# Expert loop of a product-key layer in a new order: the gathered rows are weighted and summed by one VectorE operation, input blocks are multiplied two blocks ahead

## Chip, cores and metric

One NeuronCore of a Trainium2 chip runs the whole program. The metric is the device time of one execution in microseconds (us), as the median over several runs. A span below is the time from the first to the last instruction of one profiled execution.

## What is computed

The reference is one layer of a mixing network over 512 tokens of width 1024 (with 256 context tokens ahead of it), followed by an expert layer and a final RMSNorm. The change touches the expert layer and nothing before it. Cut to that layer:

```python
def peer_ffn(u, w_q, sub_keys, u_tab, v_tab):      # 512 tokens, 16384 experts
    ...                                            # 128 experts idx and weights g for each token
    act = gelu(einsum('tkd,td->tk', u_tab[idx], t))
    return einsum('tk,tkd->td', g * act, v_tab[idx])
...
h = h + g2 * peer_ffn(u, ...)
return rmsnorm(h, final_g)
```

All arithmetic is float32. Each expert has one row of 1024 numbers in `u_tab` (dotted with the token) and one in `v_tab` (added to the token's result with its weight).

## The kernel before

**Two ways through the experts.** Three of the four groups of 128 tokens (TD = 384 tokens) take the dense way: all 16384 experts are multiplied, in 128 blocks `a` of 128 experts. For a block, TensorE computes `pu`, the product of the block's u rows with the 384 tokens; ScalarE applies gelu, giving `act`; VectorE multiplies by `gd`, the sparse matrix of routing weights; the product `ww` is then the stationary operand with which the block's v rows are added to six accumulators `pv` in PSUM (3 token groups by 2 halves). The fourth group of 128 tokens takes the sparse way: for each of its 128 slots `k`, a gather brings one row of u and v (2 x 1024 numbers) for each of the 128 tokens, VectorE dots the u half (`g_dot`), ScalarE applies gelu (`g_act`), VectorE multiplies by the routing weight (`g_weight`, a 128x1 operation), ScalarE scales the v half and GpSimd adds it to `accG` (`g_acc`). Then the next gather is issued on GpSimd's queue (`g_load`, 4 row buffers).

**Float32 by three products.** TensorE multiplies each float32 operand as a high part and a low part: `split` (lines 175 to 184) lets ScalarE write the high part (line 177) and VectorE subtract it from the full value (line 180, the low part). `mm3` issues three matmuls: high by high, low by high, high by low (lines 187 to 189). So a block costs 3 x 8 = 24 matmuls of 384 columns for `pu` and 3 x 6 = 18 of 512 columns for `pv`.

**Blocks done ahead.** The list `AHEAD` holds 70 of the 128 blocks, spread evenly. Their `act` was computed in earlier stages while TensorE had room and lies in DRAM (`act_d`); in the loop it is loaded as `acl`. The other 58 blocks compute `pu` in the loop. Two blocks outside `AHEAD` never follow each other; at eleven places two blocks of `AHEAD` do.

**Stage `weights_T`, about 955 to 1164 us.** It builds the routing matrix in 12 quarters of four steps each; a step makes one-hot operands on VectorE (`oi`, line 1557, and `ow`, line 1561), 16 small matmuls (`gdps`), and copies on ScalarE. Three steps of each quarter also run one u block ahead. The sparse way handles one slot per quarter here (slots 0 to 11).

**The expert loop, about 1169 to 2016 us.** It runs over the blocks `i` with the order on every engine fixed by the order of the calls (`manual_schedule`). In iteration `i` the kernel before calls: `e_load(i+4)` and `e_weights(i+2)` (loads on SP's queue; `gd` for four blocks at a time); for about one slot `k` in each iteration `g_dot`, `g_act`, `g_weight`; the splits of u block `i+2` and v block `i+1`; `e_u(i+1)` (the u product and its gelu); `e_w(i+1)` (times `gd`, and split); `g_acc(k)` and `g_load(k+4)`; and last `e_v(i)`. So the v product of block `i` in an iteration needs the `ww` made one iteration earlier, and that `ww` needs a `pu` computed in that same earlier iteration. The raw loads use a ring of 10 buffers, the split blocks a ring of 6, `acl` has 3 tiles, and `gd` alternates between two.

Of the kernel before, what the change touches and what calls it, by code (L numbers as in the profile page):

```python
# [7 lines left out]
F32 = mybir.dt.float32  # L8
# [4 lines left out]
AF = mybir.ActivationFunctionType  # L13
ALU = mybir.AluOpType
# [3 lines left out]
P = 128  # L18
# [132 lines left out]
def build(tc, A, out, dbg=None):  # L151
# [23 lines left out]
    def split(hi, lo, full, eng=None, lows=None):  # L175

        S.activation(hi, full, AF.Copy)  # L177

        def low():
            (eng or V).tensor_tensor(lo, full, hi.bitcast(F32), ALU.subtract)  # L180
        if lows is None:
            low()
        else:
            lows.append(low)
# [1021 lines left out]
        for t in range(NX):  # L1206
            out_mm(accs[t], w, kk, t, i == 0, False)
    ld, sp = {}, {}
    FIRST = [(0, 1), (1, 0), (1, 1), (2, 0)]

    def e_fetch(a, i):
        ld[a, i] = wload(A["peer_ut"][a] if i == 0 else A["peer_uv"][a * P:(a + 1) * P, D:2 * D])

    def e_split(a, i, eng=None, lows=None):
        sp[a, i] = wspl(ld[a, i], (KB, 2)[i], eng, lows)
# [301 lines left out]

    def g_act(k):
        S.activation(actG[:, k:k + 1], actG[:, k:k + 1], AF.Gelu)  # L1519

    def g_weight(k):
        V.tensor_tensor(wG[:, k:k + 1], actG[:, k:k + 1], gG[:, k:k + 1], ALU.mult)  # L1522

    def g_acc(k):
        row = rows.pop(k)
        S.activation(row[:, D:2 * D], row[:, D:2 * D], AF.Copy, scale=wG[:, k:k + 1])  # L1526
        if k:
            G.tensor_tensor(accG, accG, row[:, D:2 * D], ALU.add)  # L1528
        else:
            G.tensor_copy(accG, row[:, D:2 * D])  # L1530


    def slots_T(t):
# [15 lines left out]
    def weights_T(t):  # L1549
        for q8 in range(16):  # L1550
            if q8 % 4 == 0:
                stg = sg.tile([P, P, TQ], F32, name="stg")

            def tb(ap):
                return ap[:, t * 16 + q8].rearrange("p w (g c) -> p (w g) c", c=2).unsqueeze(2).broadcast_to([P, 8, P, 2])
            oi = gs2.tile([P, 2, 4, P, 2], F16, name="oi", bufs=3)
            V.tensor_tensor(oi.rearrange("p w g b c -> p (w g) b c"), iotaA.unsqueeze(1).broadcast_to([P, 8, P, 2]), tb(ixT), ALU.is_equal)  # L1557
            ob, oa = oi[:, 0], oi[:, 1]
            ow = gs2.tile([P, 2, 4, P, 2], F16, name="ow", bufs=3)
            for w in range(2):  # L1560
                V.tensor_tensor(ow[:, w], oa, tb(gwT)[:, w * 4:w * 4 + 4], ALU.mult)  # L1561
            oh, ol = ow[:, 0], ow[:, 1]
            for q4 in range(2):
                ps = psD.tile([P, 4, P], F32, name="gdps")
                for j in range(4):
                    tt = q4 * 4 + j
                    pr, c = tt // 2, tt % 2
                    PE.matmul(ps[:, j, :], ob[:, pr, :, c], oh[:, pr, :, c], start=True, stop=False)
                    PE.matmul(ps[:, j, :], ob[:, pr, :, c], ol[:, pr, :, c], start=False, stop=True)  # L1569
                t0 = q8 % 4 * 8 + q4 * 4  # L1570
                S.activation(stg[:, :, t0:t0 + 4].rearrange("p a t -> p t a"), ps, AF.Copy, scale=1.0 / GSCALE)  # L1571
            if q8 % 4 == 3:
                nc.scalar.dma_start(gd_d[t * 4 + q8 // 4], stg)
            if q8 in UQ:
                next(ahead, None)
            k = t * 4 + q8 // 4
            gq[0] = stg
            if q8 % 4 == 0:
                if k:
                    g_acc(k - 1)  # L1580
                    g_load(k + 3)
                g_dot(k)
            elif q8 % 4 == 1:
                g_act(k)
            elif q8 % 4 == 3:
                g_weight(k)

    UQ = (0, 1, 3, 4, 5, 7, 8, 9, 11, 12, 13, 15)

# [51 lines left out]
    gls = [gl]  # L1641
    psV = ep.ps("psV", bufs=1)
    accT = [[psV.tile([P, 512], F32, name=f"pv{t}{hf}") for hf in range(2)] for t in range(3)]
    ac, ww, gw, sqs, fss = {}, {}, {}, {}, {}

    def e_load(a):
        if a in AHEAD:
            ac[a] = gl.tile([P, TD], F32, name="acl")
            nc.sync.dma_start(ac[a], act_d[AHEAD.index(a)])
        elif (a, 0) not in ld:  # L1650
            e_fetch(a, 0)
        if (a, 1) not in ld:
            e_fetch(a, 1)

    def e_split_u(a):
        if (a, 0) not in sp:
            e_split(a, 0)

    def e_split_v(a):
        if (a, 1) not in sp:  # L1660
            e_split(a, 1)

    def e_weights(a):
        if a % 4 == 0:
            n = NQ if a else NQ - 1
            gd = gls[a // 4 % 2].tile([P, NQ, 4 * TQ], F32, name="gd", bufs=1)
            nc.sync.dma_start(gd[:, 0:n, :], gd_d[0:n, :, a:a + 4, :].rearrange("q b a t -> b q (a t)"))
            if n < NQ:
                G.tensor_copy(gd[:, n, :], gq[0][:, 0:4, :].rearrange("p a t -> p (a t)"))
            gq[0] = gd  # L1670
        gd = gq[0][:, :, a % 4 * TQ:(a % 4 + 1) * TQ]
        gw[a] = gd

    def e_u(a):
        if a in AHEAD:
# [3 lines left out]
        S.activation(ac[a], pu[:, :TD], AF.Gelu)  # L1679

    def e_w(a):
        x = ac.pop(a)
        xq = x.rearrange("p (q t) -> p q t", q=NQ)
        V.tensor_tensor(xq, xq, gw.pop(a), ALU.mult)  # L1684
        wh = ex.tile([P, TD], F32R, name="wwh", bufs=3)
        wl = ex.tile([P, TD], F32R, name="wwl", bufs=3)
        split(wh, wl, x)
        ww[a] = (wh, wl)

    def e_v(a, t, hfs=(0, 1)):  # L1690
# [52 lines left out]
    def within(f, i):  # L1743
        if 0 <= i < P:
            f(i)
    LAST = 3
    kG = [12 + min(P - 12, (i * (P - 12) + 121) // 122) for i in range(P + 1)]
    with tc.manual_schedule():
        e_weights(0)
        sgp.close()  # L1750
# [2 lines left out]
        g2r = e1.tile([P, D], F32, name="g2r")  # L1753
        fgr = e1.tile([P, D], F32, name="fgr")
        hx = e1.tile([P, NX, D], F32, name="hx")
        for i in range(-4, P + 1):
            within(e_load, i + 4)
            if i > -2:
                within(e_weights, i + 2)
            now = range(kG[i], kG[i + 1]) if 0 <= i < P else ()  # L1760
            for k in now:
                g_dot(k)
                g_act(k)
                g_weight(k)
            within(e_split_u, i + 2)
            within(e_split_v, i + 1)
            within(e_u, i + 1)
            within(e_w, i + 1)
            for k in now:
                g_acc(k)  # L1770
                g_load(k + 4)
            if 0 <= i < P - LAST:
                for t in range(3):
                    e_v(i, t)
                del ww[i]
            if i == 64:
                f_load()
            if i == P - 4:
                f_mul(3, 0)
                f_mul(3, 1)  # L1780
            if i == P - 3:
                f_sq(3, 0)
                f_sq(3, 1)
                f_gain(3, 0)
                f_gain(3, 1)
            if i == P - 1:
                S.activation(e1.tile([P, 1], F32, name="warm"), epsc, AF.Sqrt)
# [49 lines left out]
```

## Time and profile before

| what | value |
|---|---|
| time, median of 3 runs (lowest to highest) | 2030.38 us (2030.21 to 2032.35) |
| the profiled execution's own time | 2030.01 us |
| its span | 2028.2 us |
| TensorE matmul busy | 1887.1 us (93%) |
| VectorE busy | 1516.8 us (75%) |
| ScalarE busy | 932.7 us (46%) |
| GpSimd busy | 914.9 us (45%) |
| mean DMA rate over the span | 220 GB/s |

PE is TensorE's matmuls, PEld its weight loads (they overlap), DVE VectorE, ACT ScalarE, POOL GpSimd, SP the engine that issues most loads. Matmuls are pipelined and the profile models their ends, so the busy share of PE hides short waits: the start times in the timeline tell more than the share does. The mean of a whole run also mixes stages with different limits; the change acts from about 955 us on. The profiled execution's time is 1.8 us above its span, and 0.4 us below the median of the runs.

### The profile page before, as it was taken

The numbers are of one execution on the slowest core, as the hardware profiler recorded it, in microseconds if no ns is written. First come the engines' busy times: TensorE is split into PE (matmuls) and PEld (weight loads), VectorE is DVE, ScalarE is ACT, GpSimd is POOL, SyncE is SP. The second block draws the span as 40 slices with busy tenths as digits, with TensorE's granted clock in tenths as the row PEclk, the third lists the DMA queues.
The fourth block names the chain that finished last, engine by engine and source line by source line (L and its number), as shares of the span: only waits on it lengthen the run. The fifth ranks groups of instructions, "written<-read, shape, count | busy, mean of one in ns | idle before, by whom it ended". The sixth has DMA issues, their size and how long they took to land.

```text
span 2028.2 us, 26813 instructions
## 1 busy us (share of the span) xinstructions
PE 1887.1 (93%) x9703; PEld 1546.4 (76%) x9703; DVE 1516.8 (75%) x2604; ACT 932.7 (46%) x1491; POOL 914.9 (45%) x458
## 2 busy tenths in 40 slices
PE   7999998879998999888999799999999999999997
PEld 4777866556777889888999677777787878778775
DVE  5552179986535456998899878888888888888885
ACT  4332233426544333433777645455445445444444
POOL 1004046740013543564122256576666575675653
PEclk9999999989999999989999789999999999999999
DMA  9546232145313433464787698888888998888971
GB/s 339 166 135 206 63 114 63 42 153 185 96 65 107 147 113 107 132 229 136 246 291 281 230 381 308 313 311 315 304 318 316 354 330 303 317 318 294 323 268 59
DMA packets 209044, 445.20 MB, mean 220 GB/s; under 512 B 13296, under 2 KB 135920, under 8 KB 190960
## 3 DMA queue, kind: packets, MB, share of 16 engines
q1 hardware_dynamic: 171616, 258.47, 39.0%
q0 software_dynamic: 18432, 134.23, 17.4%
q10 hardware_dynamic: 18864, 50.80, 6.7%
q8 instruction: 76, 1.25, 0.2%
q14 instruction: 56, 0.46, 0.1%
HBM read 394.02 MB, written 51.51 MB: 220 GB/s over the span
## 4 chain that ended last, share of the span: by engine, by line
PE 36%; DVE 29%; issue 17%; ACT 8%; DMA 6%; POOL 3%; ACTq 0%; DVEq 0%; SPq 0%; POOLq 0%
DVE wl L180 10%; DVE row L1516 6%; PE acc L187 4%; PE acc L189 4%; PE acc L188 4%; PE pu L189 3%; PE pu L187 3%; PE pu L188 3%; POOL wl L180 3%; ACT wwh L177 3%; DMA wraw<-in_peer_ut 2%; DVE oi L1557 2%; ACT wh L177 2%; DVE ow L1561 1%; PE acc L419 1%
## 5 line engine op out<-in xcount | busy, mean ns | idle before, releaser
L1528 POOL TENSOR_TENSOR accG<-accG,row 128x1024 f32<-128x1024 f32 x127 | 358.7, 2825 | 383.8 <-ACT row L1526 379.3
L180 DVE TENSOR_TENSOR wl<-wraw,wh 128x1024 fp32r<-128x1024 f32 x268 | 339.5, 1283 | 149.0 <-ACT wh L177 140.4
L177 ACT ACTIVATE wh<-wraw 128x1024 fp32r<-128x1024 f32 x324 | 335.1, 1051 | 227.3 <-PE acc L188 80.0
L189 PE MATMUL pu<-u2h,wl 128*128 128x384 f32 (+2 forms) x1040 | 360.9, 347 | 15.1 <-DVE wl L180 12.7
L187 PE MATMUL pu<-u2h,wh 128*128 128x384 f32 (+2 forms) x1040 | 359.3, 346 | 16.0 <-ACT act L1303 14.6
L188 PE MATMUL pu<-u2l,wh 128*128 128x384 f32 (+2 forms) x1040 | 354.8, 341 | 0.0
L187 PE MATMUL pv<-wh,wwh 128*128 128x512 f32 x768 | 310.0, 404 | 25.1 <-ACT wwh L177 24.8
L189 PE MATMUL pv<-wh,wwl 128*128 128x512 f32 x768 | 309.7, 403 | 0.0
L188 PE MATMUL pv<-wl,wwh 128*128 128x512 f32 x768 | 303.7, 395 | 0.0
L1522 DVE TENSOR_TENSOR wG<-actG,gG 128x1 f32<-128x1 f32 x128 | 223.2, 1744 | 33.0 <-ACT actG L1519 33.0
L1511 POOL DMA_INDIRECT row<-in_peer_uv,idxG x128 | 210.9, 1648 | 36.2 <-POOL accG L1528 33.1
L189 PEld LDWEIGHTS pu<-u2h,wl 128*128 128x128 f32 x1040 | 199.8, 192 | 32.2 <-DVE wl L180 28.1
L180 POOL TENSOR_TENSOR wl<-wraw,wh 128x1024 fp32r<-128x1024 f32 x56 | 143.7, 2570 | 166.3 <-ACT wh L177 139.6
L187 PEld LDWEIGHTS pu<-u2h,wh 128*128 128x128 f32 x1040 | 200.3, 193 | 20.2 <-ACT act L1303 15.9
L187 PEld LDWEIGHTS pv<-wh,wwh 128*128 128x128 f32 x768 | 144.9, 189 | 76.6 <-ACT wwh L177 49.7
L188 PEld LDWEIGHTS pu<-u2l,wh 128*128 128x128 f32 x1040 | 200.2, 193 | 2.5
L189 PEld LDWEIGHTS pv<-wh,wwl 128*128 128x128 f32 x768 | 144.7, 188 | 48.5 <-DVE wwl L180 16.6
L188 PEld LDWEIGHTS pv<-wl,wwh 128*128 128x128 f32 x768 | 144.9, 189 | 29.6 <-issue 0.2
L1516 DVE CUSTOM_DVE_ANT_0 row<-row,u2G 128x1024 f32<-128x1024 f32 x128 | 156.1, 1219 | 0.0
L1526 ACT ACTIVATE row<-row,wG 128x1024 f32<-128x1024 f32 x128 | 145.7, 1138 | 4.7 <-ACT act L1303 3.8
L177 ACT ACTIVATE wwh<-acl 128x384 fp32r<-128x384 f32 x70 | 36.7, 525 | 197.0 <-DVE acl L1684 197.0
L1571 ACT ACTIVATE stg<-gdps 128x512 f32<-128x512 f32 x96 | 96.8, 1137 | 17.7 <-PE gdps L1569 17.3
(412 smaller groups left out, 3346.0 us busy)
## 6 DMA issues: line engine op xcount, KB each, us to landing
wraw<-in_peer_ut SPq DMA_DIRECT2D x128, 512.0 KB, 4.6
wraw<-in_peer_uv SPq DMA_DIRECT2D x128, 512.0 KB, 6.3
gd_d<-stg ACTq DMA_DIRECT2D x12, 2048.0 KB, 8.4
gd<-gd_d SPq DMA_DIRECT2D x31, 768.0 KB, 9.1
wraw<-in_w_in SPq DMA_DIRECT2D x36, 512.0 KB, 4.1
acl<-act_d SPq DMA_DIRECT2D x70, 192.0 KB, 5.6
act_d<-act ACTq DMA_DIRECT2D x68, 192.0 KB, 3.8
kT<-in_ada_w SPq DMA_DIRECT2D x18, 512.0 KB, 4.6
```

The source lines that it names most:

```text
L177: S.activation(hi, full, AF.Copy)
L180: (eng or V).tensor_tensor(lo, full, hi.bitcast(F32), ALU.subtract)
L187: PE.matmul(ps, ah, bh, start=start, stop=False)
L188: PE.matmul(ps, ah, bl, start=False, stop=False)
L189: PE.matmul(ps, al, bh, start=False, stop=stop)
L1511: G.indirect_dma_start(out=rows[k], out_offset=None, in_=A["peer_uv"], in_offset=bass.IndirectOffsetOnAxis(ap=idxG[:, k:k + 1], axis=0))
L1516: V.tensor_tensor_reduce(row[:, 0:D], row[:, 0:D], u2G, 1.0, 0.0, ALU.mult, ALU.add, actG[:, k:k + 1])
L1522: V.tensor_tensor(wG[:, k:k + 1], actG[:, k:k + 1], gG[:, k:k + 1], ALU.mult)
L1526: S.activation(row[:, D:2 * D], row[:, D:2 * D], AF.Copy, scale=wG[:, k:k + 1])
L1528: G.tensor_tensor(accG, accG, row[:, D:2 * D], ALU.add)
L1557: V.tensor_tensor(oi.rearrange("p w g b c -> p (w g) b c"), iotaA.unsqueeze(1).broadcast_to([P, 8, P, 2]), tb(ixT), ALU.is_equal)
L1571: S.activation(stg[:, :, t0:t0 + 4].rearrange("p a t -> p t a"), ps, AF.Copy, scale=1.0 / GSCALE)
```

## The change

The sparse way loses three operations and gets others. VectorE no longer multiplies the 128x1 weight; ScalarE does, as a copy with a per-partition scale, right behind its gelu. ScalarE no longer scales the 1024-wide v half and GpSimd no longer adds it: one VectorE `scalar_tensor_tensor` multiplies the v half by the weight and adds `accG`. GpSimd keeps only the gathers. The slots are spread over 121 iterations in place of 122.

The loop gets a new order. u blocks (or `acl`) are loaded 6 iterations ahead, v blocks still 4, `gd` 5 in place of 2. u blocks are split at `i+3` in place of `i+2`, and `e_u` multiplies block `i+2` in place of `i+1`. `e_w(i+1)` comes first in the iteration, ahead of the dot. All high parts of an iteration are called before its low parts, which VectorE now does in the order ww, u, v. The list `FIRST`, the pieces that are loaded and split before the loop, no longer holds u block 2 (which is in `AHEAD`, so it was never multiplied) but u block 3.

```diff
-    FIRST = [(0, 1), (1, 0), (1, 1), (2, 0)]
+    FIRST = [(1, 0), (0, 1), (3, 0), (1, 1)]
...
     def g_act(k):
         S.activation(actG[:, k:k + 1], actG[:, k:k + 1], AF.Gelu)
-
-    def g_weight(k):
-        V.tensor_tensor(wG[:, k:k + 1], actG[:, k:k + 1], gG[:, k:k + 1], ALU.mult)
+        S.activation(wG[:, k:k + 1], actG[:, k:k + 1], AF.Copy, scale=gG[:, k:k + 1])
 
     def g_acc(k):
         row = rows.pop(k)
-        S.activation(row[:, D:2 * D], row[:, D:2 * D], AF.Copy, scale=wG[:, k:k + 1])
         if k:
-            G.tensor_tensor(accG, accG, row[:, D:2 * D], ALU.add)
+            V.scalar_tensor_tensor(accG, row[:, D:2 * D], wG[:, k:k + 1], accG, ALU.mult, ALU.add)
         else:
-            G.tensor_copy(accG, row[:, D:2 * D])
+            V.tensor_scalar(accG, row[:, D:2 * D], wG[:, k:k + 1], None, ALU.mult)
...
                 g_dot(k)
             elif q8 % 4 == 1:
                 g_act(k)
-            elif q8 % 4 == 3:
-                g_weight(k)
...
-    def e_load(a):
-        if a in AHEAD:
+    def e_load(a, i):
+        if i == 0 and a in AHEAD:
             ac[a] = gl.tile([P, TD], F32, name="acl")
             nc.sync.dma_start(ac[a], act_d[AHEAD.index(a)])
-        elif (a, 0) not in ld:
-            e_fetch(a, 0)
-        if (a, 1) not in ld:
-            e_fetch(a, 1)
+        elif (a, i) not in ld:
+            e_fetch(a, i)
...
+    def e_high(a, i):
+        if (a, i) in ld and (a, i) not in sp:
+            lows[a, i] = []
+            e_split(a, i, None, lows[a, i])
+
+    def e_low(a, i):
+        for f in lows.pop((a, i), ()):
+            f()
...
     def e_w(a):
         x = ac.pop(a)
         ...
-        split(wh, wl, x)
+        lows[a, 2] = []
+        split(wh, wl, x, None, lows[a, 2])
...
-        for i in range(-4, P + 1):
-            within(e_load, i + 4)
-            if i > -2:
-                within(e_weights, i + 2)
+        for i in range(-6, P + 1):
+            within(lambda a: e_load(a, 0), i + 6)
+            within(lambda a: e_load(a, 1), i + 4)
+            if i > -5:
+                within(e_weights, i + 5)
             now = range(kG[i], kG[i + 1]) if 0 <= i < P else ()
+            within(e_w, i + 1)
             for k in now:
                 g_dot(k)
+            within(lambda a: e_high(a, 0), i + 3)
+            within(lambda a: e_high(a, 1), i + 1)
+            within(lambda a: e_low(a, 2), i + 1)
+            within(lambda a: e_low(a, 0), i + 3)
+            within(lambda a: e_low(a, 1), i + 1)
+            for k in now:
                 g_act(k)
-                g_weight(k)
-            within(e_split_u, i + 2)
-            within(e_split_v, i + 1)
-            within(e_u, i + 1)
-            within(e_w, i + 1)
+            within(e_u, i + 2)
             for k in now:
                 g_acc(k)
                 g_load(k + 4)
```

## Rows read from the trace of the kernel before

**Rows 1.** Busy by stretch, 1200 to 1950 us: pu's instructions, then pv's.

```profile
1200.00:1950.00 750.00, 237.83 (x1232) 215.11 (x1230) 25.76 (x54) 1.00 0.89 316
...
1200.00:1950.00 750.00, 506.15 (x2050) 376.80 (x2051) 0.00 (x0) 1.00 0.89 316
```

**Rows 2.** Timeline of PE (start us, us long): first, some middle and last rows.

```profile
1169.33 0.79 PE L187 MATMUL pv<-wh,wwh 128*128 128x512 f32 x1 [7.24 <-ACT wwh L177]
...
1187.79 0.40 PE L187 MATMUL pv<-wh,wwh 128*128 128x512 f32 x1
...
1196.19 0.34 PE L187 MATMUL pu<-u2h,wh 128*128 128x384 f32 x1
...
1200.41 0.40 PE L187 MATMUL pv<-wh,wwh 128*128 128x512 f32 x1
...
2015.33 0.40 PE L189 MATMUL pv<-wh,wwl 128*128 128x512 f32 x1
```

**Rows 3.** Waits of PEld, 1200 to 1950 us: total us, times, longest.

```profile
PEld pv L187 <- ACT wwh L177: 36.8, 52, 2.0
PEld pu L189 <- DVE wl L180: 23.4, 44, 0.6
PEld pv L189 <- DVE wwl L180: 15.4, 52, 0.3
```

**Rows 4.** Timeline of DVE, ACT and POOL around 1500 us.

```profile
1497.30 1.99 ACT L177 ACTIVATE wh<-wraw 128x1024 fp32r<-128x1024 f32 x2
...
1499.37 2.35 DVE L180 TENSOR_TENSOR wl<-wraw,wh 128x1024 fp32r<-128x1024 f32 x2
...
1503.25 1.22 DVE L1516 CUSTOM_DVE_ANT_0 row<-row,u2G 128x1024 f32<-128x1024 f32 x1
...
1503.87 2.86 POOL L1528 TENSOR_TENSOR accG<-accG,row 128x1024 f32<-128x1024 f32 x1 [2.46 <-ACT row L1526]
...
1504.75 2.00 DVE L1522 TENSOR_TENSOR wG<-actG,gG 128x1 f32<-128x1 f32 x1 [0.27 <-ACT actG L1519]
...
1506.68 1.21 DVE L180 TENSOR_TENSOR wl<-wraw,wh 128x1024 fp32r<-128x1024 f32 x1
...
1507.00 1.71 POOL L1511 DMA_INDIRECT row<-in_peer_uv,idxG  x1 [0.27 <-POOL accG L1528]
...
1507.81 0.55 DVE L1684 TENSOR_TENSOR act<-act,gd 128x384 f32<-128x384 f32 x1
...
1508.39 0.53 ACT L177 ACTIVATE wwh<-act 128x384 fp32r<-128x384 f32 x1 [2.34 <-DVE act L1684]
...
1508.95 0.56 DVE L180 TENSOR_TENSOR wwl<-act,wwh 128x384 fp32r<-128x384 f32 x1 [0.59 <-ACT wwh L177]
```

**Rows 5.** Lines 1522, 585 and 1519 by themselves: duration ns min/median/max, first and last start.

```profile
L1522 DVE TENSOR_TENSOR wG<-actG,gG x128: 151/2007/2025, 973.7 to 1967.8; 128x1 f32<-128x1 f32 x128
...
L585 DVE SCALAR_TENSOR_TENSOR c<-xp,colv,c x12: 1015/1022/1023, 66.0 to 171.1; 128x770 f32<-128x770 f32 x12
...
L1519 ACT ACTIVATE actG<-actG x128: 192/203/207, 973.5 to 1967.5; 128x1 f32<-128x1 f32 x128
```

**Rows 6.** Timeline of a quarter of weights_T.

```profile
1110.46 3.44 DVE L1557 TENSOR_TENSOR oi<-iotaA,ixT 128x2048 f16<-128x2048 f16 x1
...
1128.03 2.49 POOL L1528 TENSOR_TENSOR accG<-accG,row 128x1024 f32<-128x1024 f32 x1 [13.30 <-ACT row L1526]
...
1128.16 3.44 DVE L1557 TENSOR_TENSOR oi<-iotaA,ixT 128x2048 f16<-128x2048 f16 x1
...
1132.39 0.23 PE L1568 MATMUL gdps<-ow,oi 128*128 128x128 f16 x1 [0.47 <-DVE ow L1561]
1132.98 0.22 PE L1569 MATMUL gdps<-ow,oi 128*128 128x128 f16 x1 [0.36 <-DVE ow L1561]
```

**Rows 7.** DMA: a stretch with more traffic, and us to landing of v loads.

```profile
1600.00:1700.00 100.00, 97.27 (x441) 79.33 (x440) 86.56 (x97) 51.17 (x76) 68.13 (x31) 1.00 0.94 340
...
wraw<-in_peer_uv SPq DMA_DIRECT2D x106, 512.0 KB, 6.3
```

More of the change, by code (lines that the diff above doesn't have):

```diff
@@ L1643, in build @@
     accT = [[psV.tile([P, 512], F32, name=f"pv{t}{hf}") for hf in range(2)] for t in range(3)]
-    ac, ww, gw, sqs, fss = {}, {}, {}, {}, {}
-    def e_load(a):
-        if a in AHEAD:
+    ac, ww, sqs, fss = {}, {}, {}, {}
+    def e_load(a, i):
+        if i == 0 and a in AHEAD:
             ac[a] = gl.tile([P, TD], F32, name="acl")
             nc.sync.dma_start(ac[a], act_d[AHEAD.index(a)])
-        elif (a, 0) not in ld:
-            e_fetch(a, 0)
-        if (a, 1) not in ld:
-            e_fetch(a, 1)
[L1655 to L1661, printed above, removed]
+        elif (a, i) not in ld:
[7 more added lines that the diff above has]
+            f()
+    lows = {}
+    gds = {}
     def e_weights(a):
@@ L1665, in e_weights @@
             n = NQ if a else NQ - 1
-            gd = gls[a // 4 % 2].tile([P, NQ, 4 * TQ], F32, name="gd", bufs=1)
+            gd = gds[a // 4] = gls[a // 4 % 2].tile([P, NQ, 4 * TQ], F32, name="gd", bufs=1)
             nc.sync.dma_start(gd[:, 0:n, :], gd_d[0:n, :, a:a + 4, :].rearrange("q b a t -> b q (a t)"))
@@ L1669, in e_weights @@
                 G.tensor_copy(gd[:, n, :], gq[0][:, 0:4, :].rearrange("p a t -> p (a t)"))
-            gq[0] = gd
-        gd = gq[0][:, :, a % 4 * TQ:(a % 4 + 1) * TQ]
-        gw[a] = gd
     def e_u(a):
@@ L1683, in e_w @@
         xq = x.rearrange("p (q t) -> p q t", q=NQ)
-        V.tensor_tensor(xq, xq, gw.pop(a), ALU.mult)
+        V.tensor_tensor(xq, xq, gds[a // 4][:, :, a % 4 * TQ:(a % 4 + 1) * TQ], ALU.mult)
         wh = ex.tile([P, TD], F32R, name="wwh", bufs=3)
         wl = ex.tile([P, TD], F32R, name="wwl", bufs=3)
-        split(wh, wl, x)
+        lows[a, 2] = []
+        split(wh, wl, x, None, lows[a, 2])
         ww[a] = (wh, wl)
@@ L1746, in build @@
     LAST = 3
-    kG = [12 + min(P - 12, (i * (P - 12) + 121) // 122) for i in range(P + 1)]
+    kG = [12 + min(P - 12, (i * (P - 12) + 120) // 121) for i in range(P + 1)]
     with tc.manual_schedule():
```

## The prediction, made before the changed kernel was seen

> **What bounds the kernel now.** I read the page's share of each engine first, then the stretches, then PE's timeline and its waits, and last the other engines' timelines inside one pair of iterations. The page calls PE 93% busy, which suggests that nothing is left; the start times say otherwise. From 1187.79 to 1196.19 us PE starts 36 pv matmuls with no wait, 0.2333 us each; from 1196.19 to 1200.41 it starts 24 pu matmuls, 0.1758 us each [rows 2]. Between 1200 and 1950 us it issues 1232 pu and 2050 pv matmuls [rows 1]: 1232 x 0.1758 + 2050 x 0.2333 = 216.6 + 478.3 = 694.9 us of work in 750. So 55.1 us, 7.3%, is lost there, at a granted clock of 1.00, that is 2.4 GHz [rows 1]. The reader is to see that PE is the bound and yet is kept waiting in nearly every pair of iterations. The weight loads name three causes: the high part of ww (ScalarE), the low part of a u block, the low part of ww (both VectorE) [rows 3]. (Their waits add up to more than 55 us, since a weight load starts ahead of the matmul before it has ended.)
>
> Why they are late stands in the timeline [rows 4]. After the dot, VectorE issues the 128x1 weight, and it lasts 2.00 us, until GpSimd's 2.86 us addition ends at 1506.73; alone it takes 0.15 [rows 5]. Behind it in VectorE's queue stand the low parts, and behind these the multiplication of a fresh `act`: 1507.81 us, with ww's high part at 1508.39 and its low part at 1508.95, where PE already waits. It is a chain inside one iteration: pu, gelu, product, high, low, pv.
>
> **The change, part by part.**
>
> *VectorE, sparse way.* Each slot loses the 2.00 us weight and gains a 1024-wide `scalar_tensor_tensor`. The trace of before has none of that size. The nearest is 770 wide, 1.02 us [rows 5]; adding 254 elements at the 1.04 ns per element of that row's neighbours (a 1024-wide low part takes 1.21 us against 0.56 for 384, so 0.65 / 640 = 1.02 ns) gives 1.28 us. Lower bound 1.21 (the plain 1024-wide subtraction), upper bound 1.21 + 1.85 = 3.06, if it were blocked as the weight is. I take 1.29: the 770-wide row is the same instruction form, and GpSimd has no additions left that could block it. So VectorE gains about 0.7 us per slot.
>
> *ScalarE* loses a 1024-wide scaling, about the 1.0 us of a 1024-wide high part [rows 4], and gets a 128x1 copy near the 0.20 us of its gelu [rows 5]. ScalarE has room either way; this counts as nothing, hidden beside VectorE's 1.29 us.
>
> *GpSimd* keeps the 1.71 us gather issue [rows 4], now behind VectorE's sum. The row it fetches is dotted four slots later, over 20 us away.
>
> *One block more of distance.* In the new order PE in iteration i needs only what the others made in iteration i-1 from a pu of iteration i-2. I lay out a pair of iterations, the first with a u block: PE 4.22 + 18 x 0.2333 = 8.42, then 4.20, together 12.62 us. VectorE's next iteration starts with the product of that u block's `act`, so at 4.22 + 0.47 (a gelu as long as the 384-wide ScalarE row, 0.53 at most) + about 0.2 = 4.9 us. Its work per iteration by [rows 4]: product 0.55, dot 1.22, ww low 0.56, v low 1.21, sum 1.29 = 4.83, and 1.21 more for a u block: 10.87 us in a pair, 86% of 12.62. Meanwhile ScalarE makes ww high (0.53), u high and v high (1.0 each) while VectorE dots, so each low part finds its high part ready or 0.1 us short. The u low part is ready at 4.9 + 0.55 + 1.22 + 0.56 + 1.21 = 8.4 us; PE wants it at 12.62. The ww of that iteration is ready before 8, wanted at 16.8. VectorE ends its second iteration at 4.9 + 10.87 = 15.8 and is let go again at 17.5. So every wait of [rows 3] has at least 4 us of cover, and where two blocks of `AHEAD` follow each other VectorE has 15.7 us of work in PE's 16.8. If the sum costs over 1.29 + (12.62 - 10.87) / 2 = 2.16 us the cover is gone and VectorE sets the pace.
>
> *Loads on SP.* u loads and `acl` are issued 6 ahead, `gd` 5, v 4 as before. With 3 `acl` tiles, the load for block i+6 waits until VectorE has taken the tile of about three `AHEAD` blocks earlier, in iteration i-1 or i, and v and `gd` loads stand behind it. `gd` waits for its tile's last product, also in i-1. That leaves a v load about three iterations, 19 us, against a median of 6.3 to land [rows 7]: nothing, with 12 us of cover. The bytes stay; in a loop 7% shorter 316 GB/s [rows 1] becomes 340, which the stretch from 1600 us already carried at a DMA share of 0.94 with PE undisturbed [rows 7]. `FIRST` trades one useless u block for u block 3: one load and one split fewer in the loop, about 1 us of VectorE, hidden.
>
> *Sum for the loop.* 55.1 us in the window. The stage runs from 1169.33 to 2015.73 us [rows 2], 96 us of it outside the window; at the same 7.3% that is 7.0. Total 62, of which I leave 2 for the start: the first pv matmuls last 0.79 instead of 0.40 us [rows 2] at 1.2 GHz after an idle PE, since the first ww hangs on loads that the change does not touch. Saved: 60 us, 64 if the edges lose more than the middle, 30 if half of the waits come back elsewhere.
>
> *Stage weights_T.* GpSimd's addition blocks one `oi` in a quarter: 3.44 us, its end set by the addition's end at 1130.5 [rows 6]; about 1.22 is its own (other steps), so 2.2 are lost. PE then waits 0.47 + 0.36 = 0.83 us for `ow` [rows 6]. VectorE gets 1.29 instead, earlier in the quarter, where the row of `ow` has about 1 us to spare. So 0.83 comes back in some 8 quarters of 17.7 us, 6.6 us, and about 0.9 in one of the two last ones, where only VectorE sets the pace (2.2 - 1.29): 7.5. Bounds 0 (the wait moves to the step behind the sum) and 12 (0.9 or a little more in all twelve).
>
> *One rule against one row.* The weight's 2.00 us beside 0.15 alone, ending with GpSimd's addition, shows that VectorE can be held for a whole GpSimd instruction [rows 4, 5]. The low part that ran from 1506.68 beside the gather issue of 1507.00 took its usual 1.21 us [rows 4], so the issue holds nothing. The Trainium skill (SBUF — State Buffer, section "Who interferes with whom") says that a VectorE instruction with two SBUF inputs contends with a GpSimd instruction that reads SBUF, and that the later one blocks fully. For the weight the trace agrees. Taken strictly for the gather issue too, which reads its indices from SBUF, it would give the last rival below, 2041 us, in place of the 1963 that the low part's row gives.
>
> *Total.* 2028.2 - 60 - 7.5 = 1960.7 us of span; 1.8 around it gives 1962.5, and the median stood 0.4 above the profiled run: **1963 us**.
>
> **The rivals.**
>
> *Half the waits return* (12%). A queue is in order, so a late gelu on ScalarE holds the next high part, and a late dot holds both. Against it: 4 us of cover. If half of the 62 stays: 1963 + 30 = 1993 us.
>
> *Loads become the wait* (5%). For it: a DMA share of 0.89 already [rows 1], and SP held by three `acl` tiles. Against it: 340 GB/s at 0.94 [rows 7]. If 316 GB/s were the ceiling the loop could not shrink at all and only weights_T's 7.5 would show: 2030.4 - 7.5 = 2023 us.
>
> *Slower: VectorE held by the gather issue* (3%). Each issue follows the sum, just where VectorE starts the next product, which has two SBUF inputs. Were it held for the 1.71 us, a pair would be 10.87 + 3.42 = 14.3 us, less about 0.07 of overlap for each of eleven starts (two low parts in 2.35 where one takes 1.21 [rows 4]) = 13.5, against 846.4 / 64 = 13.2 now. The loop would take 64 x 13.5 = 864, 18 us more: 2030.4 + 18 - 7.5 = 2041 us. It turns slower than before from a hold of about 1.5 us. Against it: the undisturbed low part above.
>
> **How the numbers follow.** The forecast holds 80%: its own range is 1950 (edges and weights_T at their best: 2030.4 - 66 - 12, and 2 for the start) to 1977 (weights_T at 0, loop 53). Adding the first rival up to 1993 brings the range to 1950 to 1993, with some 1 in 10 left out above and little below. I call 0.2%, 4 us, about what a measurement of this kernel can tell from no change. Faster holds the forecast, the half and most of the loads' case (at 2023 us it is 0.36% faster): 80 + 12 + 3 = 95%. Same: the rest of the loads' case, 2%. Slower: 3%.
>
> **What would show it.** Right: PE starts from the loop's second block on at 0.233 and 0.176 us with no waits of weight loads on wwh, wl or wwl; VectorE about 85% busy with gaps in front of the product of a fresh `act`; its sum near 1.29 us; DMA near 340 GB/s; quarters of weights_T near 16.8 us; loop near 786 us. Wrong: the sum above 2.16 us, or lengthened beside a gather issue; PE waiting for DMA; PE's granted clock below 1.00 in the loop; quarters still at 17.7.

## The result, and the profile after

The changed kernel takes **1978.86 us** (median of 4 runs, 1975.43 to 1979.52) against 2030.78 us for the kernel before on the same chip: a ratio of 0.974, 95% interval 0.9723 to 0.9757. The prediction said 1963 us and 1950 to 1993. The saving is 51.9 us where 67 were expected, and the stages show that this is not one shortfall but several differences, one of them the other way (spans of the profiled executions, us):

| stage | before | after | change | predicted |
|---|---|---|---|---|
| to the first `oi` of weights_T | 957.9 | 961.1 | +3.1 | 0 |
| weights_T, first `oi` to last `gdps` | 203.8 | 206.5 | +2.7 | -7.5 |
| PE idle before the first pv | 7.55 | 16.67 | +9.1 | 0 |
| loop, first pv to the end of the last | 846.4 | 780.5 | -65.9 | -60 |
| end of the last pv to the end of the span | 12.5 | 12.0 | -0.5 | 0 |

The first row is not the change's: up to there all fourteen kernels of this case run the same instructions, and their profiled executions take 955.1 to 964.5 us for them (956.1 and 956.6 in two that have the new sparse way). In weights_T the five kernels with the old sparse way take 203.8 to 204.9 us, and the six with that of the kernel after 205.8 to 206.9.

First the loop. Busy time by stretch of the kernel after: pu's instructions (PE, PEld, ACT, then granted clock, DMA share, GB/s), then pv's; and below a stretch of all engines (PE, PEld, DVE, ACT, POOL):

```profile
1200.00:1900.00 700.00, 229.72 (x1252) 221.52 (x1252) 26.82 (x54) 1.00 0.93 343
...
1200.00:1900.00 700.00, 487.11 (x2058) 385.69 (x2057) 0.00 (x0) 1.00 0.93 343
```

```profile
1500.00:1600.00 100.00, 100.00 (x470) 85.79 (x469) 80.15 (x104) 41.42 (x81) 15.81 (x17) 1.00 0.98 367
```

Counted as in [rows 1]: 1252 x 0.1758 + 2058 x 0.2333 = 700.2 us of work in 700. Nothing is lost any more. The waits of PEld between 1200 and 1900 us, all of them, beside [rows 3]:

```profile
PEld pu L187 <- ACT g2r L1093: 0.7, 1, 0.7
PEld pu L1091 <- issue: 0.5, 2, 0.2
```

The three releasers of [rows 3] are gone. DMA carries 367 GB/s at a share of 0.98 with PE full, above the 340 of [rows 7].

A pair of iterations on VectorE and ScalarE in the kernel after (timeline), beside [rows 4]:

```profile
1505.88 0.55 DVE L1680 TENSOR_TENSOR acl<-acl,gd 128x384 f32<-128x384 f32 x1
1506.35 1.22 DVE L1516 CUSTOM_DVE_ANT_0 row<-row,u2G 128x1024 f32<-128x1024 f32 x1
...
1506.52 0.53 ACT L177 ACTIVATE wwh<-acl 128x384 fp32r<-128x384 f32 x1 [2.59 <-DVE acl L1680]
...
1507.49 0.55 DVE L180 TENSOR_TENSOR wwl<-acl,wwh 128x384 fp32r<-128x384 f32 x1
1508.03 2.36 DVE L180 TENSOR_TENSOR wl<-wraw,wh 128x1024 fp32r<-128x1024 f32 x2
1510.30 1.28 DVE L1525 SCALAR_TENSOR_TENSOR accG<-row,wG,accG 128x1024 f32<-128x1024 f32 x1
...
1513.64 1.23 DVE L180 TENSOR_TENSOR wl<-wraw,wh 128x1024 fp32r<-128x1024 f32 x1
1514.78 1.28 DVE L1525 SCALAR_TENSOR_TENSOR accG<-row,wG,accG 128x1024 f32<-128x1024 f32 x1
1518.27 0.56 DVE L1680 TENSOR_TENSOR act<-act,gd 128x384 f32<-128x384 f32 x1 [2.21 <-ACT act L1674]
```

ScalarE makes ww's high part while VectorE dots, so `wwl` starts with no wait; VectorE's only gap, 2.21 us here, is in front of a fresh `act`, where the prediction put it. The sum by itself (duration ns min/median/max), beside [rows 5]:

```profile
L1525 DVE SCALAR_TENSOR_TENSOR accG<-row,wG,accG x127: 1276/1279/1282, 1002.1 to 1915.1; 128x1024 f32<-128x1024 f32 x127
```

1.279 us against the 1.29 predicted, and 1.282 at most.

Now what went the other way. A quarter of weights_T in the kernel after (timeline), beside [rows 6]:

```profile
1104.80 3.96 ACT L1568 ACTIVATE stg<-gdps 128x512 f32<-128x512 f32 x4
...
1109.16 1.06 ACT L177 ACTIVATE wh<-wraw 128x1024 fp32r<-128x1024 f32 x1 [0.40 <-ACT stg L1568]
...
1110.26 1.23 DVE L180 TENSOR_TENSOR wl<-wraw,wh 128x1024 fp32r<-128x1024 f32 x1 [2.50 <-ACT wh L177]
1111.40 1.28 DVE L1525 SCALAR_TENSOR_TENSOR accG<-row,wG,accG 128x1024 f32<-128x1024 f32 x1
1112.60 1.22 DVE L1516 CUSTOM_DVE_ANT_0 row<-row,u2G 128x1024 f32<-128x1024 f32 x1
...
1113.74 1.22 DVE L1554 TENSOR_TENSOR oi<-iotaA,ixT 128x2048 f16<-128x2048 f16 x1
```

No `oi` is held any more, but the sum now stands right behind a low part that waits 2.50 us for ScalarE, and the dot, `oi` and `ow` follow it. The quarters in the middle last 18.2 us (dot to dot) instead of 17.7; the last two get shorter, 14.5 and 12.2 us against 15.6 and 13.1. And the start of the loop (timelines of POOL, SP, DVE and PE):

```profile
1167.56 0.94 POOL L1511 DMA_INDIRECT row<-in_peer_uv,idxG  x1 [8.06 <-DVE accG L1525]
...
1167.93 0.38 SPq L1665 DMA_DIRECT2D gd<-gd_d  x1
...
1183.10 0.56 DVE L1680 TENSOR_TENSOR acl<-acl,gd 128x384 f32<-128x384 f32 x1 [15.81 <-DMA acl<-act_d]
...
1184.27 0.80 PE L187 MATMUL pv<-wh,wwh 128*128 128x512 f32 x1 [16.36 <-ACT wwh L177]
```

The gather for slot 15 goes out 0.4 us ahead of the load of `gd(0)`. Before, GpSimd's last addition kept it back until 5.4 us behind that load (1167.52 against 1162.12). The first product waits for `gd(0)` and for `acl(0)`, which was issued 0.4 us behind it and landed 0.5 us behind it; its row names the later one. PE waits 16.36 us here, from the end of the last `gdps` (the table counts from its start); its row in [rows 2] says 7.24.

### The profile page after: what moved, and what is told of

Its sections match the earlier page's. It is cut to its first block, busy times and chain, and to the rows that moved or that the text cites. A ratio compares the mean times of both kernels' runs of the same rounds, so it can differ in the third digit from the quotient of the medians.

```text
span 1976.8 us, 26304 instructions
## 1 busy us (share of the span) xinstructions
PE 1852.5 (94%) x9703; PEld 1557.8 (79%) x9703; DVE 1417.2 (72%) x2604; ACT 829.2 (42%) x1491; POOL 476.9 (24%) x330
## 4 chain that ended last, share of the span: by engine, by line
PE 72%; DVE 12%; issue 6%; ACT 5%; POOL 3%; DMA 1%; ACTq 0%; SPq 0%; POOLq 0%; DVEq 0%
PE pv L187 9%; PE pv L188 9%; PE pv L189 9%; PE pu L187 6%; PE pu L189 6%; PE pu L188 6%; PE acc L187 4%; PE acc L189 4%; PE acc L188 4%; POOL wl L180 3%; ACT stg L1568 2%; PE acc L419 2%; DVE wl L180 1%; PE acc L421 1%; PE acc L423 1%
## 5 line engine op out<-in xcount | busy, mean ns | idle before, releaser
L180 DVE TENSOR_TENSOR wl<-wraw,wh 128x1024 fp32r<-128x1024 f32 x268 | 331.6, 1255 | 150.0 <-ACT wh L177 149.7
L189 PE MATMUL pu<-u2h,wl 128*128 128x384 f32 (+2 forms) x1040 | 355.6, 342 | 4.5 <-DVE wl L180 2.5
L1511 POOL DMA_INDIRECT row<-in_peer_uv,idxG x128 | 133.6, 1043 | 804.3 <-DVE accG L1525 768.6
L187 PE MATMUL pv<-wh,wwh 128*128 128x512 f32 x768 | 303.9, 396 | 16.4 <-ACT wwh L177 16.4
L189 PE MATMUL pv<-wh,wwl 128*128 128x512 f32 x768 | 303.5, 395 | 0.0
L187 PEld LDWEIGHTS pu<-u2h,wh 128*128 128x128 f32 x1040 | 200.4, 193 | 19.7 <-ACT act L1303 16.4
L1525 DVE SCALAR_TENSOR_TENSOR accG<-row,wG,accG 128x1024 f32<-128x1024 f32 x127 | 162.4, 1279 | 0.0
L1680 DVE TENSOR_TENSOR act<-act,gd 128x384 f32<-128x384 f32 x58 | 33.5, 578 | 142.3 <-ACT act L1674 142.3
L1674 ACT ACTIVATE act<-pu 128x384 f32<-128x384 f32 x58 | 28.6, 492 | 226.6 <-PE pu L189 226.6
```

Of the source, the lines that this page charges most:

```text
L187: PE.matmul(ps, ah, bh, start=start, stop=False)
L189: PE.matmul(ps, al, bh, start=False, stop=stop)
L1511: G.indirect_dma_start(out=rows[k], out_offset=None, in_=A["peer_uv"], in_offset=bass.IndirectOffsetOnAxis(ap=idxG[:, k:k + 1], axis=0))
L1525: V.scalar_tensor_tensor(accG, row[:, D:2 * D], wG[:, k:k + 1], accG, ALU.mult, ALU.add)
L1680: V.tensor_tensor(xq, xq, gds[a // 4][:, :, a % 4 * TQ:(a % 4 + 1) * TQ], ALU.mult)
```

## The experiments

Twelve kernels ran, each timed beside the kernel before.

**The two halves.** `e5` has the new order of the loop and the old sparse way, `e4` the new sparse way and the old order.

The first diff below is against the kernel after, the second against the kernel before.

```diff
-        S.activation(wG[:, k:k + 1], actG[:, k:k + 1], AF.Copy, scale=gG[:, k:k + 1])
+    def g_weight(k):
+        V.tensor_tensor(wG[:, k:k + 1], actG[:, k:k + 1], gG[:, k:k + 1], ALU.mult)
...
+        S.activation(row[:, D:2 * D], row[:, D:2 * D], AF.Copy, scale=wG[:, k:k + 1])
-            V.scalar_tensor_tensor(accG, row[:, D:2 * D], wG[:, k:k + 1], accG, ALU.mult, ALU.add)
+            G.tensor_tensor(accG, accG, row[:, D:2 * D], ALU.add)
...
```

```diff
-    def g_weight(k):
-        V.tensor_tensor(wG[:, k:k + 1], actG[:, k:k + 1], gG[:, k:k + 1], ALU.mult)
+        S.activation(wG[:, k:k + 1], actG[:, k:k + 1], AF.Copy, scale=gG[:, k:k + 1])
...
-        S.activation(row[:, D:2 * D], row[:, D:2 * D], AF.Copy, scale=wG[:, k:k + 1])
-            G.tensor_tensor(accG, accG, row[:, D:2 * D], ALU.add)
+            V.scalar_tensor_tensor(accG, row[:, D:2 * D], wG[:, k:k + 1], accG, ALU.mult, ALU.add)
...
```

> The changed kernel with the sparse way of before (weight on VectorE, scaling on ScalarE, addition on GpSimd), so the new loop order alone. Theory (VectorE is still held about 1.9 us per slot by GpSimd's addition, now at another instruction; 12.4 us of work in a pair of 12.6, less the overlap of neighbours): the waits go nearly all, the loop takes 782 to 795 us, quarters stay at 17.7 and the start idle near 7.5 us; 1965 to 1978 us, no slower than the whole change. Rival (without the fused sum VectorE sets the pace): the loop takes over 810 us, 1990 us or more.

> The kernel before with the sparse way's part of the change alone: weight on ScalarE, one fused sum on VectorE, old loop order. Theory of the chain (the 2.0 us hold and the 0.27 us wait ahead of it leave VectorE's queue, and the 1.29 us sum stands at its end, behind the low part of ww): PE's 68 us of waits in the loop fall under 15, the loop takes about 795 us; quarters of weights_T 18.2; about 1990 us in all. Rival (the second block of distance is what counts): half of the waits stay, the loop takes over 810 us, 2010 us or more.

The order alone: 1964.99 us (1962.12 to 1965.91), ratio 0.9673 (0.9655 to 0.969); loop 780.9, quarters 17.66, PE idle 7.67. It takes the whole gain of the loop and beats the whole change by 13.9 us. The sum alone: 2094.85 us, ratio 1.0319 (1.0299 to 1.0338); loop 898.0. The same edit that costs the new order nothing in the loop costs the old order 52 us there, a miss of over 100 us. VectorE and ScalarE in `e4` (timeline of a pair of iterations, up to the next dot):

```profile
1500.25 1.22 DVE L1516 CUSTOM_DVE_ANT_0 row<-row,u2G 128x1024 f32<-128x1024 f32 x1
...
1501.51 0.20 ACT L1519 ACTIVATE actG<-actG 128x1 f32<-128x1 f32 x1 [2.96 <-DVE actG L1516]
...
1503.02 2.36 DVE L180 TENSOR_TENSOR wl<-wraw,wh 128x1024 fp32r<-128x1024 f32 x2 [1.54 <-ACT wh L177]
1505.30 0.55 DVE L1679 TENSOR_TENSOR acl<-acl,gd 128x384 f32<-128x384 f32 x1
1506.44 0.56 DVE L180 TENSOR_TENSOR wwl<-acl,wwh 128x384 fp32r<-128x384 f32 x1 [0.59 <-ACT wwh L177]
1506.91 1.28 DVE L1525 SCALAR_TENSOR_TENSOR accG<-row,wG,accG 128x1024 f32<-128x1024 f32 x1
1508.11 1.22 DVE L1516 CUSTOM_DVE_ANT_0 row<-row,u2G 128x1024 f32<-128x1024 f32 x1
...
1514.84 1.22 DVE L1516 CUSTOM_DVE_ANT_0 row<-row,u2G 128x1024 f32<-128x1024 f32 x1
```

Its queue goes out to ScalarE and back twice in an iteration: 1.54 us for the high parts, which stand behind a gelu that waits for the dot, and 0.59 for ww's. Nothing in the queue fills these trips, and the pair from 1500.25 to 1514.84 takes 14.59 us. In the kernel before, the held weight of 2.00 us [rows 4] lay over the first trip.

**Is it the place of the gelu?** `e7` is `e4` and `e13` is the kernel before, each with the gelu (and weight) behind the splits; `e16` is the changed kernel with it ahead of them.

In `e7` (and `e13`, with `g_weight(k)` behind `g_act(k)` in both places), and then in `e16`:

```diff
                 g_dot(k)
-                g_act(k)
             within(e_split_u, i + 2)
             within(e_split_v, i + 1)
+            for k in now:
+                g_act(k)
```

```diff
                 g_dot(k)
+                g_act(k)
             within(lambda a: e_high(a, 0), i + 3)
...
-            for k in now:
-                g_act(k)
             within(e_u, i + 2)
```

> The sum alone in the old order (which took 2094.85 us), with one move: ScalarE's gelu and weight of the slot stand behind the high parts of u and v instead of ahead of them. Theory, that the sum alone was slow because ScalarE's queue waited for the dot with the high parts behind it, so that VectorE's low parts waited 1.5 us twice in an iteration pair: the waits go, a pair falls from 14.6 to 12.9 to 13.3 us, the loop from 898 to 825 to 850, time 2015 to 2050 us. Rival, that the 1.28 us of the sum on VectorE are themselves too much in the old order: loop within 10 us of 898, time over 2080 us.

> The kernel before with one move and nothing else: in the loop the slot's gelu (ScalarE) and weight (VectorE) are called behind the splits of u and v instead of ahead of them; GpSimd's addition and the distance of one block stay. Theory, that the loop of before lost its 62 us since the high parts of ScalarE's queue stood behind a gelu that waits for VectorE's dot, and not through the distance nor through the 2.00 us weight as such: loop 781 to 790 us, weights_T as before, time 1964 to 1975 us. Rival, that the 2.00 us weight, now in front of the product, costs as much there as in front of the low parts: loop 815 to 850, time 2000 to 2032 us.

> The changed kernel with one move: in the loop the slot's gelu and weight on ScalarE are called right behind the dot, ahead of the high parts, as in the order before; the distance of two blocks stays. Theory, that the distance alone also suffices, since VectorE's waits for the late high parts (some 0.9 us an iteration, a pair from 9.83 to 11.6 us) stay under PE's 12.2 us: loop 780 to 785, time 1976 to 1982 us. Rival, that the place of the gelu is all that counts: pair over 12.6 us, loop over 805, time over 2003 us.

`e7`: 1980.99 us (1979.96 to 1983.85), ratio 0.9756 (0.974 to 0.9773), loop 784.1. One moved call takes 114 us off `e4`, far more than expected, and brings the loop to within 4 us of the changed kernel's with a distance of one block. `e13`: 2025.08 us, ratio 0.9969 (0.9959 to 0.9979), loop 839.6: the theory that the place of the gelu alone lost the 62 us falls. `e16`: 1978.26 us, ratio 0.9746 (0.9727 to 0.9764), loop 781.5: in the new order the place no longer shows in the time. In `e13` the hold has only moved (timeline of POOL and DVE):

```profile
1498.27 2.86 POOL L1528 TENSOR_TENSOR accG<-accG,row 128x1024 f32<-128x1024 f32 x1 [2.53 <-ACT row L1526]
...
1499.17 3.04 DVE L180 TENSOR_TENSOR wl<-wraw,wh 128x1024 fp32r<-128x1024 f32 x1 [0.29 <-ACT wh L177]
1502.14 0.15 DVE L1522 TENSOR_TENSOR wG<-actG,gG 128x1 f32<-128x1 f32 x1
```

The weight takes its 0.15 us, and the low part behind the addition 3.04 instead of 1.21. In `e5` it is `wwl` that lasts 2.61 us. The Trainium skill (SBUF — State Buffer, "Who interferes with whom") says that a VectorE instruction with two SBUF inputs contends with a GpSimd instruction that reads SBUF and that whoever comes later blocks; all three places agree.

What sorts these kernels is one account of VectorE's queue. All its waits between 1200 and 1900 us (total us, times, longest) in the kernel before, in `e13`, in `e7` and in the kernel after:

```profile
DVE wwl L180 <- ACT wwh L177: 62.7, 106, 0.6
DVE wG L1522 <- ACT actG L1519: 27.8, 101, 0.8
DVE wl L180 <- ACT wh L177: 11.1, 10, 1.4
```

```profile
DVE wwl L180 <- ACT wwh L177: 63.2, 107, 0.6
DVE wl L180 <- ACT wh L177: 36.8, 103, 1.6
```

```profile
DVE wwl L180 <- ACT wwh L177: 67.4, 114, 0.6
DVE act L1679 <- ACT act L1674: 63.2, 51, 3.5
DVE wl L180 <- ACT wh L177: 2.9, 1, 2.9
```

```profile
DVE act L1680 <- ACT act L1674: 128.0, 52, 3.7
DVE wwl L180 <- ACT wwh L177: 5.7, 5, 3.3
DVE wl L180 <- ACT wh L177: 2.0, 5, 0.4
```

By the windows view VectorE was busy for 598.75 of these 700 us before. With the waits, 598.75 + 62.7 + 27.8 + 11.1 = 700.4, that is all of the time. That sum says nothing by itself, since work and waits fill the time of any engine; what tells is whom the waits are for. Every one is a short trip to ScalarE, and none is for the gelu of a fresh `act`, behind which stands PE. So VectorE's queue set the pace, at a busy share of 86% (in which the held weight is counted as busy). In `e13` the same: 600.24 + 100.0. In `e7` and after, 63.2 and 128.0 us are waits for `act`: VectorE has time left, and PE sets the pace. The same account for seven kernels, 1200 to 1900 us. The 700 us hold between 100 iterations (`e4`) and 115 (after), so the last column gives the queue's need in us per iteration: busy time and trips, divided by 700, times the loop, divided by 128.

| kernel | order, sum, gelu | VectorE busy | trips to ScalarE | wait for `act` | loop | busy and trips, per iteration |
|---|---|---|---|---|---|---|
| before | old, on GpSimd, early | 598.8 | 101.6 | 0 | 846.4 | 6.62 |
| `e13` | old, on GpSimd, late | 600.2 | 100.0 | 0 | 839.6 | 6.56 |
| `e4` | old, fused, early | 496.1 | 205.3 | 0 | 898.0 | 7.03 |
| `e7` | old, fused, late | 566.4 | 70.3 | 63.2 | 784.1 | 5.57 |
| `e5` | new, on GpSimd, late | 669.2 | 6.0 | 19.3 | 780.9 | 5.88 |
| after | new, fused, late | 564.3 | 7.7 | 128.0 | 780.5 | 4.98 |
| `e16` | new, fused, early | 568.0 | 124.2 | 8.4 | 781.5 | 6.04 |

PE's floor is 57 u blocks x 24 x 0.1758 + 128 x 18 x 0.2333 = 778 us, 6.08 an iteration. The four kernels whose queue needs less than that wait for `act` and are within 7 us of the floor; the three others need more, never wait for `act`, and are 62 to 120 us above it.

**How much room is left?** `e6` makes a second sum of the same size in each slot of the loop, into the row's own tile, beside the right one.

```diff
     def g_acc(k):
         row = rows.pop(k)
+        if k >= 12:
+            V.scalar_tensor_tensor(row[:, 0:D], row[:, D:2 * D], wG[:, k:k + 1], row[:, 0:D], ALU.mult, ALU.add)
```

> The changed kernel with a second fused sum of the same size in each slot of the loop, into the row's own tile: 1.28 us more for VectorE in each of 116 slots, with no other change. By the durations that the prediction added up a pair becomes 10.87 + 2.56 = 13.4 us, over PE's 12.62, the loop 64 x 13.4 = 860 and the time about 2058 us. By the busy share after (0.806 of the 12.2 us pair, 9.83 us, since instructions overlap) it becomes 12.39 us, just over PE's pair: loop 790 to 800, time 1985 to 2000 us. If VectorE had more room than both: 1979 us.

1979.47 us (1976.44 to 1981.13), ratio 0.9747 (0.9731 to 0.9763): nothing lost, loop 781.8. VectorE is busy 692.83 of 700 us and waits 2.0 for `act`; that is just the end of its room. The prediction's limit of 2.16 us for the sum was too low, since durations overlap: in the rows of the kernel after, the dot of 1.22 us is followed 1.14 later by the next instruction, and the low part of 1.23 at 1513.64 by the sum at 1514.78.

**Where the 14 us against the order alone went.** `e9` keeps the old sparse way for the twelve slots of weights_T and fuses the sum in the loop only. `e2` is the changed kernel with gather 15 kept back until the first ww is ready.

In `e9` against `e5`, and in `e2` against the kernel after:

```diff
     def g_acc(k):
         row = rows.pop(k)
+        if k >= 12:
+            V.scalar_tensor_tensor(accG, row[:, D:2 * D], wG[:, k:k + 1], accG, ALU.mult, ALU.add)
+            return
...
             for k in now:
                 g_act(k)
-                g_weight(k)
+                S.activation(wG[:, k:k + 1], actG[:, k:k + 1], AF.Copy, scale=gG[:, k:k + 1])
```

```diff
     g_acc(11)
-    g_load(15)
...
+            if i == -1:
+                G.tensor_copy(e1.tile([P, 1], F32, name="hold"), ww[0][1][:, 0:1].bitcast(F32))
+                g_load(15)
```

> New order, and the fused sum for the 116 slots of the expert loop only; the twelve slots of weights_T keep the old way (weight on VectorE, scaling on ScalarE, addition on GpSimd). Theory, that within the new order the fused sum neither gains nor costs in the loop, and all of its cost lies in weights_T and at the start: quarters 17.7, idle 7.6, loop 781 us, time 1963 to 1967 us, the same as the order alone. Rival, that part of the cost comes from the loop itself: 1972 to 1979 us.

> The changed kernel, with the gather of slot 15 held on GpSimd's queue until the first ww is made, by a 128x1 copy that reads it. Theory (that gather, 1 MB, now starts 0.4 us ahead of the first gd load and shares the DMA engines with it, where in the kernel before it started 5.4 us behind): PE's idle time ahead of the first pv falls from 16.6 to 8 to 11 us, 1971 to 1974 us in all. Rival (the store of the last quarter and the other loads do it): the idle time stays above 15 us, 1978 us.

`e9`: 1965.2 us (1962.75 to 1968.78), ratio 0.968 (0.9664 to 0.9696), quarters 17.7, idle 7.5, loop 781.0: as the theory said, the fused sum neither gains nor costs inside the loop, and the whole loss lies ahead of it. `e2`: 1968.31 us (1965.61 to 1969.47), ratio 0.9686 (0.967 to 0.9703); idle 7.25 instead of 16.67, quarters still 18.2. The DMA issues of 1160 to 1190 us (KB, us to landing) in the kernel after, then in `e2`:

```profile
gd<-gd_d SPq DMA_DIRECT2D x1, 704.0 KB, 14.5
```

```profile
gd<-gd_d SPq DMA_DIRECT2D x1, 704.0 KB, 5.1
```

So the 9.1 us at the start are the gather's: shown by holding it back and nothing else. Of the 14.4 us between the spans of the kernel after and `e5`, 9.0 lie at the start, 2.8 in weights_T, and 3.0 ahead of it, where both run the same instructions. Three kernels tried another place for the sum in weights_T: `e1` ahead of the block split in the first step, `e11` in the third step of its own quarter, `e14` in the fourth.

`e1`, and then `e11` (`e14` has 3 in place of 2):

```diff
-            if q8 in UQ:
-                next(ahead, None)
...
                 g_dot(k)
-            elif q8 % 4 == 1:
+            if q8 in UQ:
+                next(ahead, None)
+            if q8 % 4 == 1:
                 g_act(k)
```

```diff
-                if k:
-                    g_acc(k - 1)
-                    g_load(k + 3)
                 g_dot(k)
             elif q8 % 4 == 1:
                 g_act(k)
+            elif q8 % 4 == 2:
+                g_acc(k)
+                g_load(k + 4)
...
-    g_acc(11)
-    g_load(15)
```

> The changed kernel with one move in weights_T: in the first step of a quarter the sum, the gather and the dot are called ahead of the u block done ahead, so on VectorE they stand before that block's low part and not behind it. Theory (the sum and the dot, 2.3 us, stand behind a low part that waits 2.5 us for ScalarE, and PE waits for the one-hot operands behind them): the quarter falls from 18.2 to about 16.6 us, PE's own pace, nine times; about 14 us off, 1965 us in all. Rival (ScalarE's extra 128x1 weight, 0.29 us ahead of four copies, or the order on PE sets the quarter): it stays above 17.8 us, 1975 us or more.

> The changed kernel with one move in weights_T: the sum (and the gather that follows it) is called in the third step of its own quarter, where no block is split ahead, instead of in the first step of the next quarter. Theory, that the sum costs 18.2 us quarters because it stands behind a low part that waits for ScalarE, and that gather 15 costs the start because it goes out together with the load of gd(0): quarters of 16.5 to 17.7 us, gather 15 out some 9 us ahead of that load, PE idle 7 to 8 us before the first pv; time 1978.9 - (5 to 12) - 9 = 1958 to 1965 us. Rival, that the quarter is set by VectorE's total work whatever the place of the sum: quarters stay at 18.2 us, only the start is gained, 1970 us.

> The changed kernel with the sum and its gather called in weights_T behind the fourth step of their own quarter (two steps behind the weight) instead of behind the first step of the next one. Theory, that the third step failed at 2021.9 us because the sum waited 4.3 us for a weight called one step before, and that one step later the weight is ready (0.6 us ahead in the trace after) while the sum fills time in which VectorE waits 2.5 us for a high part: quarters 16.8 to 17.6 us, gather 15 some 5 us ahead of the load of gd(0), idle 8 to 12 us, time 1963 to 1972 us. Rival, that it waits for the weight again: a wait of over 1 us ahead of the sum, quarters of 18.2 us or more, over 1975 us.

All three missed. `e1`: 1982.47 us, ratio 0.9751 (0.9721 to 0.978), quarters 18.5 to 19.7. `e11`: 2021.9 us, ratio 0.9946 (0.993 to 0.9963), quarters 22 to 23.7; gather 15 went out only 4 us ahead of the load and PE still idled 12.1. `e14`: 1981.29 us, ratio 0.9758 (0.9742 to 0.9775), quarters 18.6 to 19.5; its gather 15 left at the same moment as after, since the last quarter's fourth step is also the end of the stage, so the start gained nothing (17.9). The rows of ScalarE and VectorE say what stood in the way (timelines of `e1`, `e14`, `e11`):

```profile
1107.63 0.49 ACT L1303 ACTIVATE act<-pu 128x384 f32<-128x384 f32 x1 [5.60 <-DMA act_d<-act]
```

```profile
1103.40 0.49 ACT L1303 ACTIVATE act<-pu 128x384 f32<-128x384 f32 x1 [3.80 <-DMA act_d<-act]
...
1104.86 1.28 DVE L1525 SCALAR_TENSOR_TENSOR accG<-row,wG,accG 128x1024 f32<-128x1024 f32 x1 [1.67 <-ACT wG L1520]
```

```profile
1095.12 1.28 DVE L1525 SCALAR_TENSOR_TENSOR accG<-row,wG,accG 128x1024 f32<-128x1024 f32 x1 [4.33 <-ACT wG L1520]
```

The sum now meets a weight that ScalarE has not made, in all twelve quarters of `e11`, in nine of `e14`, in five of `e1` (there for 1.1 us at most): ScalarE's queue is at a u block's gelu, which waits for PE, or for its `act` tile's last store to land. Which of these sets 18.2 us in the kernel after stays open. That the new sparse way in this stage is the cause is shown by `e9` and `e5`, which put the old one back there; whether its sum on VectorE or its weight on ScalarE does it, no kernel tried apart.

**The best version.** `e15` is `e5` with u block 3 split and multiplied ahead of the first pv, while PE waits for `gd(0)`.

```diff
+            if i == -2:
+                e_high(3, 0)
+                e_low(3, 0)
...
-            within(e_u, i + 2)
+            if i != 1:
+                within(e_u, i + 2)
+            if i == -1:
+                e_u(3)
```

> The order alone with the old sparse way (it took 1964.99 us), and block 3 of u, split during the wait for gd(0), multiplied ahead of the first pv instead of in the loop. Theory: PE idles 7.7 us there, so the 4.2 us of that block are hidden; loop 776 to 777 us, time 1958 to 1962 us. Rival, that its splits or its gelu delay the first ww by as much: 1963 to 1967 us.

1966.85 us (1960.88 to 1971.04), ratio 0.9685 (0.9657 to 0.9713): not told apart from `e5`. In the profile the loop is shorter (778.3) and the first pv later (1172.07 against 1169.54). So the fastest median is that of the order alone, 1964.99 us, with `e9` beside it.

## Why the prediction came out as it did

- **The loop: right in size, and partly for another reason.** 65.9 us came back where 60 were named: 62 less 2 reserved for the start. Waits, busy share (81% against 85%), sum and DMA rate came as listed. But the step "It is a chain inside one iteration: pu, gelu, product, high, low, pv" does not hold as the cause: before, VectorE never waited for that gelu, and `e7` keeps these steps in one iteration and comes within 4 us of the changed loop. What bound the loop was VectorE's own queue with its trips to ScalarE, 6.6 us an iteration against PE's 6.08. The new order helps because `wwl` and the low parts find their high parts ready: the trips fall from 101.6 to 7.7 us. With the gelu early (`e16`) they are still 124.2 us, and the queue fits under PE's pace, barely, since the held weight is gone. Whether the second block of distance or the order of the calls does it, no kernel tried alone. And one reading was short: the first pv matmuls are slow at 1.2 GHz, but not only "after an idle PE"; the granted clock was 0.50 already from 1145 us on, while PE still ran `gdps`.
- **The 2.00 us weight.** It was a real load on that queue, but removing it alone was no gain: it covered the trip for the high parts, which came out as 1.5 us an iteration in `e4`. With the gelu moved as well (`e7`) both go.
- **weights_T, mis-sized: -7.5 predicted, +2.7 measured.** The step was that the sum stands "earlier in the quarter, where the row of `ow` has about 1 us to spare". VectorE's work in the stage did fall, from 188.0 to 178.2 us, but its waits for high parts rose from 11.5 to 26.4 us, and PE's for `ow` from 19.9 to 23.0: the sum stands behind a low part that waits 2.50 us for ScalarE. The lower bound given, 0, already left out a loss, and the sign of being wrong, "quarters still at 17.7", was passed.
- **The start, missed: 0 predicted, +9.1 measured.** That "the first ww hangs on loads that the change does not touch" forgot what shares DMA with them. The prediction costed the gather's queue in the loop and not at the seam between the stages, where the addition had kept it back by 5.4 us.
- **The rivals.** None came. Half the waits: none are left. Loads: 367 GB/s at 0.98, PE full. VectorE held by the gather issue: the sum never exceeds 1.282 us, and the dot beside an issue keeps 1.22.
- **The total.** 2028.2 + 3.1 + 2.7 + 9.1 - 65.9 - 0.5 = 1976.7 of 1976.8 us span. The point was 16 us too low, and the forecast's own range, 1950 to 1977, was missed by 2 us. That the stated range held is luck: its upper end was set for waits in the loop that did not return, and the start and weights_T used that room.

## What to carry to other kernels

Sort an engine's waits in the stage by whom they are for: if none is for the engine called the bound, this queue sets the pace, whatever its busy share, and each round trip in it costs as much as work does. Two edits that each look like a saving can be worth +63 and -67 us alone (each against the kernel before on its chip) and -52 together, so price an edit on the queue as the other edit leaves it. And at the seam of two stages list every transfer that an earlier release would let out, since what had kept it back may have been protecting the first load of the next stage.

## What was not expected of the hardware

- One gather out 0.4 us ahead of the 704 KB load of `gd(0)` took that load from 5.1 us (held back) to 14.5.
- The issue of a gather on GpSimd takes 0.94 us where VectorE runs nothing as it starts (51 times in the loop of the kernel after). Started inside a VectorE instruction with two SBUF inputs, it lasts about 0.82 us longer than what is left of that instruction: 1.01 us with 0.20 left (59 times there), 1.71 with 0.88 left (110 times in the loop of the kernel before, one in [rows 4]). VectorE loses nothing by it: a dot that starts during the issue keeps 1.22 us.
- An addition on GpSimd (2.86 us, 2.56 in `e5`) keeps a two-input VectorE instruction that comes after its start waiting until it has ended, whatever that instruction is: a weight of 0.15 us took 2.00, a low part of 1.21 took 3.04, a `wwl` of 0.56 took 2.61. The price, 1.83 to 2.05 us, follows what is left of the addition, not the length of the instruction.
